# Root mean squares of five norms through split sums and Ln/Exp instead of Sqrt, reciprocal and a diagonal tile

## The chip, the cores and the metric

The kernel runs on one core of a Trainium2 chip. The metric is the device time of one execution, in microseconds. Five engines matter: TensorE (PE; its weight loads are listed as PEld), VectorE (DVE), ScalarE (ACT), GpSimd (POOL) and SyncE (SP). Each works through its own instructions in order, and they wait for each other through semaphores. DMAs are issued from the queues of SP, ACT and POOL.

## The reference

A residual stream x of 1024 tokens by 1024 features passes through two layers. Layer 0 mixes with a short gated convolution, layer 1 with dilated attention, and after each comes a SwiGLU FFN. A root-mean-square norm stands ahead of each of these four parts, and a fifth at the end:

```python
def rms_norm(x, g):
    xf = x.astype(jnp.float32)
    y = xf * lax.rsqrt(jnp.mean(xf * xf, axis=-1, keepdims=True) + EPS)
    return (y * g.astype(jnp.float32)).astype(x.dtype)

def reference(x, mix_norm, ffn_norm, final_norm, ...):
    for i in range(DEPTH):
        h = rms_norm(x, mix_norm[i])
        if i % N_MIXERS == 0:
            x = x + short_conv_mixer(h, conv_w_in[j], conv_kernel[j], conv_w_out[j])
        else:
            x = x + dilated_attention_mixer(h, attn_w_qkv[j], attn_w_out[j], rel_bias)
        h = rms_norm(x, ffn_norm[i])
        x = x + swiglu(h, ffn_w_gate[i], ffn_w_up[i], ffn_w_down[i])
    return rms_norm(x, final_norm)
```

All of it is float32. Per token the norm needs one number, 1/rms (called rstd below).

## The kernel before

Activations lie transposed: a tile has 128 features on its partitions and the tokens along its columns, so x is eight tiles of 128x1024. [...]

Every dense product keeps float32 precision with split operands: a tile t becomes a high part (a copy by ScalarE into the rounded type fp32r, L142) and a low part (t minus the high part, by VectorE, L143), and a product is three matmuls, high by high, high by low and low by high (L570 to L572 in `mm`, L370 to L372 in `product`). A further scheme, in the manner of Strassen and Winograd (class `Strassen`), makes seven block products out of eight; the sums of blocks that it needs are VectorE's work (L190), as are the sums of its results (L580), while ScalarE saves banks to tiles (L576).

The order of the work is written out by hand. `unit_order` lists the products of a stage; after each product a callback (`start`, `filled`, `idle`) issues a fixed portion of the other engines' work, and `ensure` splits weights a few products ahead. The engines then run in that order, and instructions wait where their data are not there. Tiles come from pools: 41 pages of 128x1024, and half tiles of 128x512 (20 of them in the first and third part of the kernel, 8 in the attention), which hold the parts of products, block sums and other passing tiles.

A norm runs in these steps. ScalarE squares x tile by tile, and the squares are added into one tile `acc` of 128x1024 by VectorE (L445) or by adding DMAs. `Norm.stats` (L464) then works in two steps, around a `yield`:

- First step. For each 128 tokens TensorE multiplies `acc` (as weights) by one column of ones (L471), which gives the sums over features with the tokens on the partitions. ScalarE takes Sqrt (L474), VectorE the reciprocal (L475), and VectorE multiplies an identity tile `eye` by it (L480), which gives diagonal tiles `diag`, 512 columns each.
- Second step. TensorE multiplies ones by `diag` in full float32 (L487), which brings 1/rms of every token to all partitions, and ScalarE copies it to `rstd` (L488).

The conv stage calls both steps for all 1024 columns at once (`gather` and `spread`, after the products (0,3) and (2,5)) and then squares rstd (L1106), which VectorE's next work needs. The query/key stage does the same after (1,2) and (3,1). Each FFN has a first half in `group1` and a second half in `feed_forward` (n == key+1 and key+2), after which `second_half` makes VectorE and ScalarE build operands from rstd (L1276, L562), and ScalarE loads the table for Silu (L1364). The attention scales its value products by `norm.r`, the small tile with tokens on the partitions (L1517).

The last norm stands in `final`. The last product group runs over column pieces of 512, 256 and 256 tokens, eight tiles n each. After each tile VectorE adds the product to x (L492), ScalarE squares it (L1957) and multiplies by the gain (L1959), and `between` adds squares and, for the piece before, issues `squared_sum` at n == 1 and `spread` at n == 3; then `some(1)` scales a finished tile by rstd (L1968) and sends it out. For the last piece the last square is summed by TensorE itself (L1984), and VectorE multiplies by the bank (L1997) directly.

ScalarE's functions come from tables, and a change of table is an instruction of its own. Three places call Sqrt or Silu on one column only to have the table there early (L1364, L1708, L2005).

Of the kernel before, what the change touches and what calls it, by code (L numbers as in the profile page):

```python
# [10 lines left out]
F32 = mybir.dt.float32  # L11
# [6 lines left out]
S = 1024  # L18
D = 1024
# [12 lines left out]
WARM = 10  # L32

# [65 lines left out]
def trunk(ctx: ExitStack, tc: tile.TileContext, x, gains_in, cwi, ck, cwo, wqkv, wo, relb,  # L99
# [27 lines left out]
    eye = consts.tile([128, 128], F32)  # L127
# [267 lines left out]
    class Norm:  # L395
# [68 lines left out]
        def stats(self, c0, c1):  # L464

            self.flush()
            w = c1 - c0
            nt = w // 128
            b = bank()
            for t in range(nt):  # L470
                nc.tensor.matmul(b[:, t:t + 1], self.acc[:, c0 + 128 * t:c0 + 128 * t + 128], ones[:, 0:1],  # L471
                                 start=True, stop=True)
            r = self.r = consts.tile([128, KT], F32, name="r", tag="r", bufs=2)
            nc.scalar.activation(r[:, :nt], b[:, :nt], AF.Sqrt, scale=1.0 / D, bias=eps)  # L474
            nc.vector.reciprocal(r[:, :nt], r[:, :nt])  # L475
            diags = []
            for p0 in range(0, nt, 4):
                n = min(4, nt - p0)
                diag = half_page("diag")
                nc.vector.tensor_tensor(out=view(diag, 0, [[128, n], [1, 128]]),  # L480
                                        in0=view(eye, 0, [[0, n], [1, 128]]),
                                        in1=view(r, p0, [[1, n], [0, 128]]), op=ALU.mult)
                diags.append((c0 + 128 * p0, 128 * n, diag))
            yield
            for p0, n, diag in diags:
                b = bank()
                nc.tensor.matmul(b[:, :n], ones, diag[:, :n], start=True, stop=True)  # L487
                nc.scalar.activation(self.rstd[:, p0:p0 + n], b[:, :n], AF.Copy)  # L488
# [8 lines left out]
    def bias_tables():  # L497
# [30 lines left out]
        nc.vector.tensor_tensor(out=d, in0=d, in1=m, op=ALU.subtract)  # L528
        nc.scalar.activation(d, d, AF.Exp)
# [590 lines left out]
    class QueryKey(Conv):  # L1120
# [43 lines left out]
        def mix(self):  # L1164
# [44 lines left out]
            def spread():  # L1209
                run(stats)  # L1210
                self.ready = True
# [263 lines left out]
    def attention(norm, qk):  # L1475
# [193 lines left out]
        def finish(p):  # L1669
# [211 lines left out]
    nc.scalar.dma_start(gains, gains_in)  # L1881

# [27 lines left out]
    nc.gpsimd.dma_start(eye, ident)  # L1910
    nc.vector.memset(ones, 1.0)
    nc.vector.memset(eps, EPS)
# [165 lines left out]
```

## Time and profile before

| | us |
|---|---|
| median of 3 runs | 2137.89 |
| lowest and highest run | 2135.56, 2138.65 |
| profiled execution | 2136.81 |
| its span | 2135.0 |
| TensorE busy | 2103.4 (99%) |
| VectorE busy | 1744.7 (82%) |
| ScalarE busy | 1009.2 (47%) |
| GpSimd busy | 256.5 (12%) |

The granted clock of TensorE is 0.996 over the span. In rows in order of time the first two numbers are an instruction's start and duration in us; behind the engine and the line stand the operation, what it writes and reads, and the shape. In square brackets is the time that the engine idled before it, and what it waited for. Rows with `x8` merge several instructions. A full float32 matmul shows as two records. In rows of groups the busy time and the mean in ns of one instruction follow the bar.

### The profile page before, as it was taken

The page shows a single profiled execution, that of the slowest core. Times are in us where ns is not written, and L with a number is a line of the kernel's source. Part 1 is how long each engine was busy: PE and PEld are TensorE (multiplying, and loading weights), DVE is VectorE, ACT ScalarE, POOL GpSimd, SP SyncE. Part 2 cuts the span into 40 slices and gives each one's busy share as a digit, 9 for nine tenths or more (in the row PEclk, how much of TensorE's full clock was granted, in tenths as well). Part 3 has the DMA queues.
Part 4 walks back from the last instruction along what each step waited for, and adds up shares of the span by engine and source line. Part 5 has one row for each costly group of instructions (what it writes and reads, how often), then busy time and mean ns, then how long its engine had stood idle before and what let it go on. Part 6 is the DMA issues. An engine that isn't in the chain of part 4 may idle for free. (4 is left out here: it accounts for less than half of the span.)

```text
span 2135.0 us, 31015 instructions
## 1 busy us (share of the span) xinstructions
PE 2103.4 (99%) x11082; PEld 1805.6 (85%) x11082; DVE 1744.7 (82%) x3273; ACT 1009.2 (47%) x1853; POOL 256.5 (12%) x375
## 2 busy tenths in 40 slices
PE   9999999999999999999999999999999999999998
PEld 7788888888888888877899998888788888888887
DVE  8898769988888888868967687777998888888876
ACT  7333426443444554446545544545543434456435
POOL 1000000110101000010322333221011101001000
PEclk9999999999999999999999999999999999999999
DMA  7322642333332576340767777765123333368432
GB/s 219 94 94 70 227 137 71 104 104 104 114 109 99 170 218 197 112 167 30 265 204 182 186 194 216 214 198 160 59 94 105 103 109 113 101 199 240 157 94 79
DMA packets 143449, 304.90 MB, mean 143 GB/s; under 512 B 48972, under 2 KB 55422, under 8 KB 143296
## 3 DMA queue, kind: packets, MB, share of 16 engines
q1 hardware_dynamic: 107488, 201.94, 31.5%
q0 software_dynamic: 28176, 86.29, 12.7%
q10 hardware_dynamic: 7632, 14.70, 1.8%
q8 instruction: 88, 1.44, 0.3%
q14 instruction: 65, 0.53, 0.1%
HBM read 212.48 MB, written 83.05 MB: 138 GB/s over the span
## 5 line engine op out<-in xcount | busy, mean ns | idle before, releaser
L572 PE MATMUL bank<-b,w 128*128 128x512 f32 x1952 | 760.9, 390 | 4.9 <-DVE w L143 4.7
L570 PE MATMUL bank<-b,w 128*128 128x512 f32 x1952 | 762.8, 391 | 2.5 <-ACT w L142 1.7
L571 PE MATMUL bank<-b,w 128*128 128x512 f32 x1952 | 760.4, 390 | 0.6 <-DVE b L881 0.6
L572 PEld LDWEIGHTS bank<-b,w 128*128 128x128 f32 x1952 | 366.4, 188 | 85.8 <-DVE w L143 9.6
L570 PEld LDWEIGHTS bank<-b,w 128*128 128x128 f32 x1952 | 366.7, 188 | 79.5 <-ACT w L142 2.8
L571 PEld LDWEIGHTS bank<-b,w 128*128 128x128 f32 x1952 | 366.7, 188 | 76.0 <-DVE b L881 1.2
L142 ACT ACTIVATE w<-combo 128x512 fp32r<-128x512 f32 (+2 forms) x488 | 249.1, 540 | 231.5 <-DVE combo L190 214.6
L143 DVE TENSOR_TENSOR w<-combo,w 128x512 fp32r<-128x512 f32 (+2 forms) x488 | 276.2, 579 | 37.8 <-ACT w L142 37.1
L576 ACT ACTIVATE part<-bank 128x512 f32<-128x512 f32 x186 | 110.8, 596 | 388.8 <-PE bank L572 385.3
L143 DVE TENSOR_TENSOR w<-raw,w 128x512 fp32r<-128x512 f32 (+2 forms) x342 | 189.6, 575 | 38.6 <-ACT w L142 38.6
L580 DVE TENSOR_TENSOR part<-part,bank 128x256 f32<-128x256 f32 (+1 forms) x366 | 170.5, 495 | 31.2 <-PE bank L572 16.7
L142 ACT ACTIVATE w<-raw 128x512 fp32r<-128x512 f32 (+2 forms) x342 | 166.7, 530 | 44.9 <-PE bank L572 12.2
L370 PE MATMUL bank<-w_hi,w 128*128 128x512 f32 (+1 forms) x400 | 153.3, 383 | 5.1 <-ACT w_hi L142 3.7
L371 PE MATMUL bank<-w_lo,w 128*128 128x512 f32 (+1 forms) x400 | 149.7, 374 | 1.2 <-DVE w_lo L143 1.2
L372 PE MATMUL bank<-w_hi,w 128*128 128x512 f32 (+1 forms) x400 | 149.7, 374 | 0.7 <-DVE w L143 0.7
L800 DVE TENSOR_TENSOR x<-x,bank 128x512 f32<-128x512 f32 x136 | 92.6, 681 | 29.2 <-PE bank L572 29.0
L492 DVE TENSOR_TENSOR x<-x,bank 128x512 f32<-128x512 f32 (+1 forms) x104 | 66.1, 641 | 56.6 <-PE bank L372 56.1
L190 DVE TENSOR_TENSOR combo<-raw 128x512 f32<-128x512 f32 (+1 forms) x172 | 111.1, 646 | 0.0
L370 PEld LDWEIGHTS bank<-w_hi,w 128*128 128x128 f32 x400 | 75.8, 189 | 18.5 <-ACT w_hi L142 3.9
L371 PEld LDWEIGHTS bank<-w_lo,w 128*128 128x128 f32 x400 | 75.7, 189 | 14.9 <-DVE w_lo L143 2.0
L372 PEld LDWEIGHTS bank<-w_hi,w 128*128 128x128 f32 x400 | 75.6, 189 | 14.8 <-DVE w L143 1.6
L563 DVE TENSOR_TENSOR b<-hin,b 128x512 fp32r<-128x512 f32 x126 | 79.5, 684 | 9.4 <-ACT b L562 9.4
(252 smaller groups left out, 3488.6 us busy)
## 6 DMA issues: line engine op xcount, KB each, us to landing
hin<-part SPq DMA_DIRECT2D x126, 256.0 KB
raw<-in_ffn_w_gate SPq DMA_DIRECT2D x44, 512.0 KB
raw<-in_ffn_w_up SPq DMA_DIRECT2D x44, 512.0 KB
part<-sum POOLq DMA_DIRECT2D x72, 256.0 KB, 2.3
raw<-in_ffn_w_down SPq DMA_DIRECT2D x48, 384.0 KB
raw<-in_attn_w_qkv SPq DMA_DIRECT2D x27, 512.0 KB
raw<-in_conv_w_in SPq DMA_DIRECT2D x24, 512.0 KB
part<-part POOLq DMA_DIRECT2D x36, 256.0 KB, 2.4
```

What stands on the lines that cost most here:

```text
L142: nc.scalar.activation(hi, src, AF.Copy)
L143: eng.tensor_tensor(out=lo, in0=src, in1=hi, op=ALU.subtract)
L190: eng.tensor_tensor(out=c, in0=a, in1=b, op=op)
L370: nc.tensor.matmul(b, whi[:, a], ahi[:, s], start=first, stop=False)
L371: nc.tensor.matmul(b, whi[:, a], alo[:, s], start=False, stop=False)
L372: nc.tensor.matmul(b, wlo[:, a], ahi[:, s], start=False, stop=last)
L570: nc.tensor.matmul(b, hi[:, a], bhi, start=start and k == 0, stop=False, skip_group_check=True)
L571: nc.tensor.matmul(b, hi[:, a], blo, start=False, stop=False, skip_group_check=True)
L572: nc.tensor.matmul(b, lo[:, a], bhi, start=False, stop=k == n - 1, skip_group_check=True)
L576: nc.scalar.activation(t, b, AF.Copy)
L580: nc.vector.tensor_tensor(out=t, in0=t, in1=b, op=ALU.add)
L800: nc.vector.tensor_tensor(out=X[n][:, half(h)], in0=X[n][:, half(h)], in1=b, op=ALU.add)
```

## The change

`stats` splits `acc` into high and low parts per 512 columns instead of summing it by TensorE. The second step, `spread_sums`, multiplies a 128x128 tile of ones in fp32r by both parts into one bank, which puts the sums over features on all partitions at once; ScalarE makes rstd from it as Ln, then Exp of -1/2 of that. Reciprocal, `diag` and the identity go. The table set that is named for Ln and Exp is loaded at the start, ahead of the Exp in `bias_tables`, and in `final`; the early Sqrt calls go. The query/key norm writes one row of rstd to DRAM and gathers it back with tokens on the partitions, for the attention's `norm.r`. In `final`, the last piece's sums up to tile 6 are split before the last tile, the last square behind it, and four matmuls add them up.

```diff
+    ones_r = consts.tile([128, 128], F32R)
-    eye = consts.tile([128, 128], F32)
...
         def stats(self, c0, c1):
             self.flush()
-            for t in range(nt):
-                nc.tensor.matmul(b[:, t:t + 1], self.acc[:, c0 + 128 * t:c0 + 128 * t + 128], ones[:, 0:1],
-                                 start=True, stop=True)
-            r = self.r = consts.tile([128, KT], F32, name="r", tag="r", bufs=2)
-            nc.scalar.activation(r[:, :nt], b[:, :nt], AF.Sqrt, scale=1.0 / D, bias=eps)
-            nc.vector.reciprocal(r[:, :nt], r[:, :nt])
...
-            for p0, n, diag in diags:
-                b = bank()
-                nc.tensor.matmul(b[:, :n], ones, diag[:, :n], start=True, stop=True)
-                nc.scalar.activation(self.rstd[:, p0:p0 + n], b[:, :n], AF.Copy)
+            parts = []
+            for p0 in range(c0, c1, HALF):
+                s = slice(p0, min(p0 + HALF, c1))
+                w = s.stop - s.start
+                parts.append((s, split(self.acc[:, s], [half_page("sum", F32R)[:, :w] for _ in range(2)])))
+            yield
+            for s, sums in parts:
+                spread_sums(self.rstd[:, s], [sums])
+
+    def spread_sums(rstd, sums):
+        w = rstd.shape[1]
+        b = bank()[:, :w]
+        terms = [t for pair in sums for t in pair]
+        for i, t in enumerate(terms):
+            nc.tensor.matmul(b, ones_r, t, start=i == 0, stop=i == len(terms) - 1)
+        nc.scalar.activation(rstd, b, AF.Ln, scale=1.0 / D, bias=eps)
+        nc.scalar.activation(rstd, rstd, AF.Exp, scale=-0.5)
...
         nc.vector.tensor_tensor(out=d, in0=d, in1=m, op=ALU.subtract)
+        nc.scalar.preload_act_table_set(LN_EXP)
         nc.scalar.activation(d, d, AF.Exp)
...
                 run(stats)
+                rms = dram.tile([1, S], F32, name="rms")
+                norm.r = consts.tile([128, KT], F32, name="r")
+                nc.gpsimd.dma_start(rms, norm.rstd[0:1, :])
+                nc.gpsimd.dma_start(norm.r, bass.AP(rms.tensor, rms.offset, [[1, 128], [128, KT]]))
...
-                    nc.scalar.activation(scratch, eps, AF.Sqrt)
...
     nc.scalar.dma_start(gains, gains_in)
+    nc.scalar.preload_act_table_set(LN_EXP)
...
-    nc.gpsimd.dma_start(eye, ident)
+    nc.vector.memset(ones_r.bitcast(F32), 1.0)
...
+            def parts(t, i):
+                s = slice(*pieces[i])
+                w = s.stop - s.start
+                return split(t[:, s], [half_page("sum", F32R)[:, :w] for _ in range(2)])
...
             def between(i, n):
-                add_squares(int(n > 0))
+                add_squares(int(n > 0 and (i, n) != (len(pieces) - 1, KT - 2)))
                 if (i, n) == (0, 5):
-                    nc.scalar.activation(scratch, eps, AF.Sqrt)
+                    nc.scalar.preload_act_table_set(LN_EXP)
                 if i and n == 1:
-                    diags.append(squared_sum(i - 1))
+                    known.append(parts(norm.acc, i - 1))
                 elif i and n == 3:
                     s = slice(*pieces[i - 1])
-                    nc.scalar.activation(norm.rstd[:, s], spread(diags.pop()), AF.Copy)
+                    spread_sums(norm.rstd[:, s], [known.pop()])
                     scale.extend((i - 1, k, norm.rstd[:, s]) for k in range(KT))
+                elif i == len(pieces) - 1 and n == KT - 2:
+                    known.append(parts(norm.acc, i))
                 some(1)
...
             last = len(pieces) - 1
-            add_squares(1)
-            diag = squared_sum(last, sums.pop()[0])
+            known.append(parts(sums.pop()[0], last))
             some(KT)
-            rstd = spread(diag)
+            rstd = norm.rstd[:, slice(*pieces[last])]
+            spread_sums(rstd, known)
             for n in range(KT):
                 scaled(last, n, rstd)
```

`LN_EXP` is the string "natural_log_exp_and_others".

More of the change, by code (lines that the diff above doesn't have):

```diff
@@ L32 @@
 WARM = 10
+LN_EXP = "natural_log_exp_and_others"
 def paired(pairs, chunk, tiles):
@@ L1994, in spread @@
-            def spread(diag):
-                b = bank()
-                w = diag.shape[1]
-                nc.tensor.matmul(b[:, :w], ones, diag, start=True, stop=True)
-                return b[:, :w]
-            diags = []
+            def parts(t, i):
+                s = slice(*pieces[i])
+                w = s.stop - s.start
+                return split(t[:, s], [half_page("sum", F32R)[:, :w] for _ in range(2)])
+            known = []
             def between(i, n):
-                add_squares(int(n > 0))
+                add_squares(int(n > 0 and (i, n) != (len(pieces) - 1, KT - 2)))
```

28 lines of the change are left out of this document (removed).

## The prediction

> **What bounds the kernel now.** I read the busy times on the page first, then the waits of TensorE, then busy time by stretch, and then the order of time round each norm.
>
> ```profile
> PE 2103.4 (99%) x11082; PEld 1805.6 (85%) x11082; DVE 1744.7 (82%) x3273; ACT 1009.2 (47%) x1853; POOL 256.5 (12%) x375
> ```
>
> ```profile
> PE bank L572 <- DVE w L143: 4.7, 6, 1.7
> ```
>
> ```profile
> 360.00:380.00 20.00, 20.00 (x89) 16.54 (x89) 20.00 (x34) 12.27 (x23) 0.77 (x2) 1.00 0.16 40
> ...
> 1020.00:1040.00 20.00, 19.42 (x83) 15.35 (x83) 19.93 (x32) 10.39 (x18) 7.44 (x14) 1.00 0.72 250
> ...
> 1520.00:1540.00 20.00, 19.02 (x84) 15.21 (x83) 20.00 (x34) 11.68 (x21) 1.68 (x3) 1.00 0.35 119
> ```
>
> TensorE (PE) is busy for 99% of the span, and its largest wait for another engine sums to 4.7 us over the whole kernel. So a TensorE instruction that goes is worth its time, as long as the others keep up. The stretches (columns: length, then busy time of PE, PEld, DVE, ACT, POOL) show where that is doubtful: behind the norms VectorE (DVE) works 19.93 to 20.00 us of 20, and in two of these three stretches TensorE is already short of full (19.42 and 19.02). ScalarE (ACT) has room everywhere.
>
> **What TensorE gives back.** These are TensorE's rows round the norms: first the conv norm, then the norm of the first FFN, then that of the second.
>
> ```profile
> 66.72 0.39 PE L572 MATMUL bank<-b,w 128*128 128x512 f32 x1
> ...
> 68.97 0.40 PE L571 MATMUL bank<-b,w 128*128 128x512 f32 x1
> ...
> 76.72 0.40 PE L572 MATMUL bank<-b,w 128*128 128x512 f32 x1
> ...
> 78.90 0.40 PE L571 MATMUL bank<-b,w 128*128 128x512 f32 x1
> ```
>
> ```profile
> 313.42 0.39 PE L372 MATMUL bank<-w_hi,w 128*128 128x512 f32 x1
> ...
> 315.10 0.39 PE L371 MATMUL bank<-w_lo,w 128*128 128x512 f32 x1
> ...
> 340.01 0.39 PE L572 MATMUL bank<-b,w 128*128 128x512 f32 x1
> ...
> 341.90 0.40 PE L571 MATMUL bank<-b,w 128*128 128x512 f32 x1
> ```
>
> ```profile
> 1496.75 0.39 PE L571 MATMUL bank<-b,w 128*128 128x512 f32 x1
> 1496.97 0.39 PE L572 MATMUL bank<-b,w 128*128 128x512 f32 x1
> 1497.20 0.95 PE L471 MATMUL bank<-ones,acc 128*128 128x1 f32 x8
> ...
> 1498.33 0.40 PE L571 MATMUL bank<-b,w 128*128 128x512 f32 x1
> ...
> 1500.65 0.40 PE L572 MATMUL bank<-b,w 128*128 128x512 f32 x1
> 1500.88 1.02 PE L487 MATMUL bank<-diag,ones 128*128 128x512 f32 x2
> ...
> 1501.98 0.40 PE L571 MATMUL bank<-b,w 128*128 128x512 f32 x1
> ```
>
> Dense matmuls on split operands start 0.22 to 0.23 us apart (1496.75, 1496.97, 1497.20); I use 0.23. From an L572 to the next-but-one product would be two steps, 0.46. What is more than that is the norm's own time. The sums of 512 columns cost 1498.33-1496.97-0.46 = 0.90, and the spread (L487, full fp32) 1501.98-1500.65-0.46 = 0.87. In their place come two split-operand matmuls of 128x512, 2 x 0.23 = 0.46. So 512 columns give TensorE 0.90+0.87-0.46 = 1.31 us.
>
> Conv, both halves at once: 2.25-0.46 = 1.79 for the sums, 2.18-0.46 = 1.72 for the spread, less 4 x 0.23: 2.59. The query/key norm has the same instructions, 2.59. First FFN: its sums took 1.68-0.46 = 1.22 and 1.89-0.46 = 1.43, waits for the last squares included, which go with them; with two spreads, 1.22+1.43+2x0.87-2x0.46 = 3.47. Second FFN: 2 x 1.31 = 2.62. Final norm, pieces of 512 and 256 before the tail: 1.31+0.65 = 1.96. TensorE's bill falls by 13.2 us.
>
> **What the reader of rstd sees.** The chain after the spread gets longer:
>
> ```profile
> 1501.94 0.60 ACT L488 ACTIVATE rstd<-bank 128x512 f32<-128x512 f32 x1 [2.97 <-PE bank L487]
> ...
> 1502.57 0.69 DVE L1276 TENSOR_TENSOR x<-x,rstd 128x512 f32<-128x512 f32 x1 [1.26 <-ACT rstd L488]
> ```
>
> ```profile
> L1632 ACT ACTIVATE lh<-lh 128x512 f32<-128x512 f32 x16 | 9.8, 615 | 0.0
> L1268 ACT ACTIVATE x<-x,gains 128x512 f32<-128x512 f32 x8 | 5.7, 708 | 0.0
> ```
>
> Before, rstd is there 1502.54-1500.88 = 1.66 after the first spread matmul starts. Ln has a bias column, so I take L1268's 0.71 for it; Exp of this size is L1632's 0.62. The second matmul starts 0.23 after the first and lasts 0.39; ACT follows a PE end by 0.04 (1501.90 to 1501.94). So 0.62+0.04+0.71+0.04+0.62 = 2.03, 0.37 later. Ln and Exp stand in line: each needs the one before.
>
> VectorE loses the reciprocal and the diag tile's 128x512 product, and gains the low part, a subtraction of the same shape and so of the same price. ScalarE gets a copy at Exp's 0.62, Ln and Exp for a small Sqrt and a copy of 0.60: at most 1.35 more per 512 columns. With ScalarE at 47% that alone costs nothing; where it counts is the 0.37.
>
> **What of it reaches the end, norm by norm.** Second FFN: the rows of 1502.57 and of 1520 to 1540 say that VectorE starts its operands when rstd comes, is full, and has TensorE waiting for it. So rstd decides, not TensorE: the first half moves it 1.31 forward, the second half's dropped sums 0.90, less 0.37: 1.84 (ends 1.84 and 2.62, TensorE's own).
>
> ```profile
> 346.13 2.50 DVE L1276 TENSOR_TENSOR x<-x,rstd 128x512 f32<-128x512 f32 x4 [0.84 <-ACT rstd L488]
> ```
>
> ```profile
> 983.46 1.28 ACT L474 ACT_TABLE_LOAD   x1
> ...
> 985.05 0.20 DVE L475 RECIPROCAL r<-r 128x8 f32<-128x8 f32 x1 [0.89 <-ACT r L474]
> ```
>
> ```profile
> 1004.63 1.41 DVE L881 SCALAR_TENSOR_TENSOR b<-x,gains,b 128x512 fp32r<-128x512 f32 x2 [1.15 <-ACT b L880]
> ```
>
> ```profile
> 1020.53 0.50 PE L572 MATMUL bank<-b,w 128*128 128x512 f32 x1 [0.46 <-DVE w L143]
> ```
>
> First FFN: rstd moves 1.22+0.87-0.46+1.43-0.37 = 2.69; TensorE 3.47 and, in 360 to 380, without a wait. The low end is what VectorE can give: 1.22-0.37 = 0.85 from the first half, the reciprocal's 0.20, and the 0.84 it idles: 1.9. I take 2.5, between, nearer to rstd's.
>
> Query/key: at 1020.53 TensorE waits for VectorE, so VectorE must move too. Its idle time before, 0.89 at 985.05 (behind the table load of 1.28, which goes) and 1.15 at 1004.63, plus the 0.20 reciprocal, allow 2.24; the low end, without the second idle time, is 1.1, the high end TensorE's 2.59. I take 2.2.
>
> Conv: VectorE's next work waits for a square of the whole rstd, and so for both halves. The second half's rstd now takes 2.03+0.04+0.71+0.04+0.62 = 3.44 from the first spread matmul; it took about 2 x 0.87+0.2+0.60 = 2.54. That is 0.9 later, so 1.79-0.9 = 0.9 at worst; TensorE gives 2.59 and never waits there. I take 2.4.
>
> ```profile
> 2107.94 0.69 DVE L1968 TENSOR_TENSOR x<-x,rstd 128x512 f32<-128x512 f32 x1 [1.17 <-ACT rstd L2010]
> ...
> 2121.27 0.42 DVE L1968 TENSOR_TENSOR x<-x,rstd 128x256 f32<-128x256 f32 x1 [1.02 <-ACT rstd L2010]
> ...
> 2124.99 0.42 DVE L492 TENSOR_TENSOR x<-x,bank 128x256 f32<-128x256 f32 x1 [0.30 <-PE bank L372]
> ...
> 2129.13 2.74 DVE L1968 TENSOR_TENSOR x<-x,bank 128x256 f32<-128x256 f32 x8
> ```
>
> ```profile
> 2125.45 0.42 ACT L1957 ACTIVATE sq<-x 128x256 f32<-128x256 f32 x1 [0.43 <-DVE x L492]
> 2125.90 0.51 ACT L1959 ACTIVATE x<-x,gains 128x256 f32<-128x256 f32 x1
> ```
>
> Final norm: here TensorE's 1.96 is lost. VectorE carries the pieces, and waits for rstd at 2107.94 and 2121.27; both waits grow by about 0.37. Before the last L492 there are now an add that waits for the square just begun, a wait for the high part, and the low part (0.3 issue): about 1.1. Two reciprocals (0.37) go, and some of the wait for each Sqrt, since TensorE is no longer in that chain (I estimate 0.4 together). 1.1+0.74-0.37-0.4 = 1.1: so much later comes the last L492. From there to the first of the last eight products it was 2129.13-2124.99 = 4.14; now: square at +0.46, gain at +0.91, the copy at +1.33 for 0.42, the low part to +2.22, matmuls to +2.55, Ln of 256 (as L1959, 0.51) to +3.10, Exp 0.42 to +3.56: 0.6 shorter. Together 0.5 later; I take a gain of -0.5, with ends -1.0 (no idle time absorbs any) and +2.0 (TensorE's).
>
> **Edits at nothing.** The load of the identity goes and a memset of ones comes ahead of any data. On the POOL queue the row and the gather of rms come in front of the stores of the query/key stage:
>
> ```profile
> 1020.91 0.59 POOL L1144 DMA_DIRECT2D kq<-kq_hi  x1 [74.22 <-ACT w L142]
> ```
>
> The queue was idle for 74.22 us until then, and rstd is there some ten us after the reciprocal at 985.05. So both transfers have some 25 us before they hold up a store, and the gathered rows are read only behind this stage. SP's queue is not touched. Of the table loads, those that a Sqrt needed go; but for the one at 983.46 they lie in idle time of ScalarE.
>
> [...] A table load takes 1.28 here and the next instruction starts at once:
>
> ```profile
> 353.12 1.28 ACT L1364 ACT_TABLE_LOAD   x1
> 354.41 0.20 ACT L1364 ACTIVATE scratch<-eps 128x1 f32<-128x1 f32 x1
> ```
>
> [...]
>
> **The sum.** 2.4+2.5+2.2+1.84-0.5 = 8.4 us off the profiled execution's 2136.81 (span 2135.0): 2128.4. That execution lies 1.1 under the median of the runs, 2137.89. The low ends, 0.9+1.9+1.1+1.84-1.0 = 4.7, give 2132.1; the high ends, 2.59+3.47+2.59+2.62+2.0 = 13.3, give 2123.5.
>
> **Rivals.** *TensorE alone decides* (2123.5): VectorE keeps up everywhere and the tail gains. For it: 99% against 82%, and hardly a wait. Against it: the three full stretches, and the wait at 1020.53.
>
> *VectorE decides* (2132.1): each norm gives only its low end. For it: stretches at 20.00 of 20. Against it: TensorE waits in them for no more than 1 us, so some slack is there.
>
> *Slower: ScalarE changes its table between Ln and Exp.* The trace shows the danger: an Exp and the Ln right behind it each needed a load of their own.
>
> ```profile
> L529 ACT ACT_TABLE_LOAD x1 | 1.3, 1283 | 0.0
> L530 ACT ACT_TABLE_LOAD x1 | 1.3, 1283 | 0.0
> ```
>
> If the set named at the start does not stay for both, 512 columns cost two loads, 2.57 us, in the chain from the spread to rstd. It counts where VectorE waits for rstd: the second half of both FFN norms and the three pieces of the last norm, 5 x 2.57 = 12.9, and up to 23 with the first halves and conv. 2128.4+12.9 to 2128.4+23 is 2141 to 2151; I take 2144. From seven loads in these places (8.4/1.28 = 6.6) the change loses. Against it: the change loads a set by name, where before the choice was free. [...]
>
> *It gains nothing* (2137): each 512 columns now hold two half tiles from the split to the spread, where one diag tile was held, out of a pool of 20 in which the products' parts live too. A product that waits for a free one could give the 8.4 back. No row shows how full the pool is.
>
> **How the numbers follow.** Less than 0.2% (4.3 us) can hardly be told from no change here. Forecast 0.58, TensorE alone 0.12, VectorE 0.13, nothing gained 0.08, table changes 0.09. The predicted time is the forecast's, 2128.4. Faster takes the forecast, TensorE alone and most of VectorE's case (below 2133.6): 0.80. Same: 0.09, from nothing gained and the slow edge of VectorE's case. Slower: 0.11, the table changes and the worst of the waits for a half tile. The range goes from 2122.5, a little past TensorE's end, to 2136.0, into the case without a gain; outside stay the table changes and some of the rest.
>
> **What would show it.** Right: two matmuls 0.23 apart in each half's place and none in the sums' place; one table load ahead of the first norm, none between Ln and Exp; about 0.37 more from the first spread matmul to rstd; a larger wait of TensorE for VectorE in the second FFN's start, 1.0 us to some 1.8; the last tile's L492 nearly as late as before. Wrong: loads between Ln and Exp; waits for half tiles round the norms; a store of keys later than 1020 behind the gather; TensorE gaining more than 2.59 at conv or less than 1.84 at the second FFN.

## The result and the profile after

| | before | after |
|---|---|---|
| median of 21 runs each, us | 2138.33 | 2134.95 |
| ratio, with its 95% interval | 1 | 0.9987 [0.998, 0.9994] |
| profiled execution, its span, us | 2136.81, 2135.0 | 2135.06, 2133.1 |
| TensorE busy, us | 2103.4 | 2096.6 |
| TensorE matmul records | 11082 | 11000 |

The kernel became faster, by 0.13% by the ratio and by 3.4 us between the medians. The forecast was 2128.4, some 8 to 10 us less than before. So the sign is right, the time lies in the range, and well over half of the gain is missing.

The page of the changed kernel has these busy times:

```profile
PE 2096.6 (98%) x11000; PEld 1800.6 (84%) x11000; DVE 1743.4 (82%) x3266; ACT 1013.7 (48%) x1861; POOL 257.4 (12%) x376
```

These are the stretches behind the three norms that the prediction showed of before, now of the changed kernel (columns: length, busy time of PE, PEld, DVE, ACT, POOL, granted clock, DMA share, GB/s):

```profile
360.00:380.00 20.00, 20.00 (x90) 16.57 (x89) 20.00 (x34) 12.58 (x24) 1.68 (x3) 1.00 0.28 88
1020.00:1040.00 20.00, 20.00 (x88) 16.20 (x88) 19.97 (x31) 10.70 (x19) 7.04 (x14) 1.00 0.76 252
1520.00:1540.00 20.00, 19.29 (x84) 15.79 (x85) 19.97 (x35) 11.20 (x22) 2.22 (x4) 1.00 0.38 132
```

They hardly moved. What TensorE waits for, over the whole changed kernel (line, releaser, us in total, times, longest), is where the loss shows:

```profile
PE bank L1570 <- ACT o L1667: 5.8, 4, 2.5
...
PE bank L482 <- ACT sum L143: 4.4, 3, 2.1
PE bank L569 <- DVE w L144: 3.8, 6, 1.1
...
PE bank L482 <- DVE sum L144: 1.3, 1, 1.3
```

The matmul of ones (now L482) waits 5.7 us for the high and low parts of the sums, about 1.9 in the first FFN and 3.7 in the last norm. The sums and spreads in whose place it stands waited 2.1 before (L471, L1982 and L1997: 0.3, 0.8 and 1.0). (In the changed kernel L143 is the high part, L144 the low part, L445 the Square, L446 the adding of squares, L191 a block sum, L483 Ln, L484 Exp, L488 the adding to x, L567 to L569 the dense products, L1969 the products of the last norm and L1970 its output DMAs.)

To see stage by stage where the time went I laid the same instructions of two traces beside each other and followed by how much the later one is ahead. The second column of numbers is the difference of the two first traces, the third the mean of three traces of the changed kernel less the mean of four of the kernel before (minus is faster):

| stage | forecast | first pair | means |
|---|---|---|---|
| start | 0 | -0.2 | -0.5 |
| conv | -2.4 | -2.6 | -2.6 |
| first FFN | -2.5 | +0.6 | +0.1 |
| bias tables | 0 | -1.2 | -1.3 |
| query/key | -2.2 | -2.1 | -2.1 |
| attention | 0 | +2.2 | +1.9 |
| second FFN | -1.84 | -1.1 | -1.1 |
| last norm | +0.5 | +2.5 | +2.5 |
| sum | -8.4 | -1.9 | -3.1 |

Conv and query/key came as forecast. Five terms did not: the first FFN, the attention, the last norm, part of the second FFN, and, to the good, the bias tables.

### The profile page after: what moved, and what is told of

Its sections match the earlier page's. It is cut to its first block, busy times and chain, and to the rows that moved or that the text cites. A ratio compares the mean times of both kernels' runs of the same rounds, so it can differ in the third digit from the quotient of the medians.

```text
span 2133.1 us, 30849 instructions
## 1 busy us (share of the span) xinstructions
PE 2096.6 (98%) x11000; PEld 1800.6 (84%) x11000; DVE 1743.4 (82%) x3266; ACT 1013.7 (48%) x1861; POOL 257.4 (12%) x376
## 3 DMA queue, kind: packets, MB, share of 16 engines
q8 instruction: 87, 1.43, 0.3%
## 4 chain that ended last, share of the span: by engine, by line
PE 41%; DVE 7%; issue 2%; ACT 2%; POOL 1%; DMA 1%; SPq 0%; DVEq 0%; ACTq 0%; POOLq 0%
PE bank L569 8%; PE bank L568 8%; PE bank L567 8%; PE bank L1643 3%; PE bank L372 2%; PE bank L373 2%; PE bank L371 2%; PE bank L659 1%; PE bank L662 1%; PE bank L661 1%; PE bank L1513 1%; PE bank L1514 1%; PE bank L1515 1%; POOL mb L1624 1%; PE bank L1571 1%
## 5 line engine op out<-in xcount | busy, mean ns | idle before, releaser
L569 PE MATMUL bank<-b,w 128*128 128x512 f32 x1952 | 761.8, 390 | 4.0 <-DVE w L144 3.8
L567 PE MATMUL bank<-b,w 128*128 128x512 f32 x1952 | 762.3, 391 | 2.8 <-ACT w L143 2.2
L569 PEld LDWEIGHTS bank<-b,w 128*128 128x128 f32 x1952 | 367.1, 188 | 84.6 <-DVE w L144 8.2
L567 PEld LDWEIGHTS bank<-b,w 128*128 128x128 f32 x1952 | 367.5, 188 | 79.6 <-ACT w L143 3.1
L143 ACT ACTIVATE w<-combo 128x512 fp32r<-128x512 f32 (+2 forms) x488 | 249.2, 540 | 232.6 <-DVE combo L191 214.2
L144 DVE TENSOR_TENSOR w<-combo,w 128x512 fp32r<-128x512 f32 (+2 forms) x488 | 277.8, 583 | 37.8 <-ACT w L143 37.0
L144 DVE TENSOR_TENSOR w<-raw,w 128x512 fp32r<-128x512 f32 (+2 forms) x342 | 190.6, 579 | 38.4 <-ACT w L143 38.4
L143 ACT ACTIVATE w<-raw 128x512 fp32r<-128x512 f32 (+2 forms) x342 | 166.9, 530 | 46.0 <-PE bank L569 11.5
L191 DVE TENSOR_TENSOR combo<-raw 128x512 f32<-128x512 f32 (+1 forms) x172 | 111.8, 650 | 0.0
L488 DVE TENSOR_TENSOR x<-x,bank 128x512 f32<-128x512 f32 (+1 forms) x104 | 66.3, 643 | 55.6 <-PE bank L373 55.3
```

The lines of the kernel that those rows point to most:

```text
L143: nc.scalar.activation(hi, src, AF.Copy)
L144: eng.tensor_tensor(out=lo, in0=src, in1=hi, op=ALU.subtract)
L191: eng.tensor_tensor(out=c, in0=a, in1=b, op=op)
L567: nc.tensor.matmul(b, hi[:, a], bhi, start=start and k == 0, stop=False, skip_group_check=True)
L569: nc.tensor.matmul(b, lo[:, a], bhi, start=False, stop=k == n - 1, skip_group_check=True)
```

## The experiments

The gains below are read in the same way, each kernel's trace against the first trace of before.

### What the chip itself scatters

The same two kernels, profiled again, so that a difference of one pair isn't taken for an effect.

> The changed kernel once more. By the two traces at hand it gained 3.0 us at the conv norm, 1.2 at the bias tables and 2.1 at the query/key norm, and gave back 0.6 at the start, 0.6 at the first FFN's norm, 2.2 within the attention and 2.2 in the last norm. Theory: the start and the attention are chance of one execution, and come out otherwise here (attention within 1 us of the length it had before), while the losses at the first FFN (0.6) and in the last norm (2.2) come again to within 0.2. Rival: the attention's loss belongs to the change (its r comes by a gather now) and comes again with 2 us or more.

> The kernel before, for one more trace of its start, its conv stage and its attention. Theory: its first trace had a short start and a short attention by chance; here the start is 0.3 to 0.8 us and the attention 0.5 to 3 us longer than there. Rival: only the changed kernel's attention is long; here start and attention are as in the first trace to within 0.4.

> A further trace of the kernel before; as for before_1. By the theory the attention's length differs from trace to trace by 1 us and more in either kernel; by the rival it repeats to within 0.4.

> A further trace of the kernel before; as for before_1. With six traces of the same attention and eleven of the changed kernels' the means can be set side by side: by the theory they lie within 1 us, by the rival 2 us or more apart.

> A third trace of the changed kernel. Theory: attention anywhere from 0.3 to 3.7 us over the first trace of the kernel before, the first FFN's norm at -0.7 or +0.7 according to whether the clock falls behind the wait, the last norm 2.2 longer as ever. Rival: the attention repeats the 2.2 and 3.4 of the first two traces to within 0.6.

Timed, the changed kernel came to 2135.52, ratio 0.998 [0.997, 0.9989]. Spans were 2135.1 and 2128.9 for the changed kernel, 2136.2, 2133.9 and 2136.8 for the one before. Within one kernel three stages scatter and the others repeat within 0.1: the start (the traces of before differ by 1.9 at 200 us; the changed kernel's stand at -0.2, +0.7 and -0.1), the attention (from 2.2 shorter to 1.5 longer than in the first trace of before, and in the changed kernel from 0.3 shorter to 3.4 longer), and, in the changed kernel alone, the first FFN (+0.6, +0.6, -1.05). So a difference at the start is chance. Conv gave 2.6 and the last norm lost 2.5 in each of the three; the 0.6 at the start, the 3.0 at conv and the 2.2 in the last norm that the expectations take are each off by 0.3 to 0.8.

### The first FFN: who waits for the split

In the changed kernel ScalarE's order in the first half, the first 512 tokens, is: Square of the newest tile, copy of the sums, Square of the next tile, Ln, Exp. ScalarE's rows of the changed kernel:

```profile
311.76 0.63 ACT L445 ACTIVATE acc<-x 128x512 f32<-128x512 f32 x1 [2.09 <-DVE x L488]
...
312.30 0.61 ACT L143 ACTIVATE sum<-acc 128x512 fp32r<-128x512 f32 x1
316.20 0.63 ACT L445 ACTIVATE acc<-x 128x512 f32<-128x512 f32 x1 [3.29 <-DVE x L488]
...
316.74 0.67 ACT L483 ACTIVATE rstd<-bank,eps 128x512 f32<-128x512 f32 x1
317.44 0.63 ACT L484 ACTIVATE rstd<-rstd 128x512 f32<-128x512 f32 x1
```

And VectorE's, of the same time:

```profile
312.95 0.69 DVE L144 TENSOR_TENSOR sum<-acc,sum 128x512 fp32r<-128x512 f32 x1 [1.22 <-ACT sum L143]
...
315.49 0.68 DVE L488 TENSOR_TENSOR x<-x,bank 128x512 f32<-128x512 f32 x1
318.11 0.75 DVE L1247 SCALAR_TENSOR_TENSOR hcol<-x,gains,rstd 128x512 f32<-128x512 f32 x1 [1.94 <-ACT rstd L484]
```

ScalarE idles 3.29 us and Ln then starts at once behind the Square, with no wait of its own: it stood in the queue behind a Square that waits for VectorE's L488, three block sums after the low part. Ln's bank was there at 314.19, 2.55 earlier:

```profile
313.56 0.63 PE L482 MATMUL bank<-sum,ones_r 128*128 128x512 f32 x2
```

VectorE, which is the pace here, idles 1.22 and then 1.94. The kernel before had the same order, with its copy to rstd behind that Square:

```profile
318.85 0.63 ACT L444 ACTIVATE acc<-x 128x512 f32<-128x512 f32 x1 [3.50 <-DVE x L492]
...
319.56 0.60 ACT L488 ACTIVATE rstd<-bank 128x512 f32<-128x512 f32 x1
```

So there too VectorE's x released rstd, and not TensorE. From the Square's start to rstd it was 1.31 (318.85 to 320.16) and is now 1.87 (316.20 to 318.07), since Ln and Exp stand where one copy stood. In the second half TensorE has the wait. Its rows:

```profile
339.37 0.50 PE L482 MATMUL bank<-sum,ones_r 128*128 128x512 f32 x1 [0.64 <-ACT sum L143]
341.13 0.71 PE L482 MATMUL bank<-sum,ones_r 128*128 128x512 f32 x1 [1.26 <-DVE sum L144]
341.63 0.63 PE L567 MATMUL bank<-b,w 128*128 128x512 f32 x1
342.06 0.63 PE L568 MATMUL bank<-b,w 128*128 128x512 f32 x1
```

Two things are seen: 1.9 us of waiting, and after it matmuls of 0.63 instead of 0.39, 0.43 apart instead of 0.23. The stretches of the first and the third trace of the changed kernel (columns: length, PE busy, granted clock, DMA share, GB/s) tell these apart:

```profile
340.00:344.00 4.00, 2.87 (x7) 0.66 0.25 43
344.00:348.00 4.00, 4.00 (x17) 0.92 0.00 0
```

```profile
340.00:344.00 4.00, 2.89 (x13) 1.00 0.25 43
344.00:348.00 4.00, 4.00 (x19) 1.00 0.02 4
```

The same wait, once with the clock granted falling to 0.66 and once without. In the first trace it is one stretch of 3.41 us at half clock, which starts 0.12 us behind the second wait's end:

```profile
341.25:344.66 3.41, 3.41 (x9) 0.50 0.00 0
```

The clock's loss is 4 x 0.34 + 4 x 0.08 = 1.7 us, and the first FFN of the two traces differs by 1.7 (+0.6 against -1.05).

Three edits try the explanation. The first moves copy, Ln and Exp ahead of the Square, in the callback that runs before it:

```diff
 # group1, added(...)
+                if j and n == i:
+                    pre.append(norm.stats(0, HALF))
+                    next(pre[0])
+                elif j and n == i + 1:
+                    run(pre.pop())
+                    pre.append(sw.first_half())
 # group1, between(...)
                 if n == i:
-                    pre.append(norm.stats(0, HALF))
-                    next(pre[0])
                     for m in (6, 7):
                         combos[i, 0](m)
-                elif n == i + 1:
-                    run(pre.pop())
-                    pre.append(sw.first_half())
```

> The changed kernel with the copy of the sums, and later Ln and Exp, issued ahead of the square of the tile at hand in the first half of both FFN norms. Theory: in ScalarE's order they stand behind a square that waits for VectorE, and VectorE then waits 1.2 us for the copy and 1.5 to 1.9 for rstd; those waits go, VectorE's chain of operands moves 1.2 to 2 us forward, and of that at least 1 us reaches the end at the first FFN. Rival: VectorE's chain has room and only TensorE's matmuls count, so the time moves by less than 0.4.

The second leaves the first half and starts the second half's split earlier, ahead of VectorE's block sums:

```diff
                     last_step()
+                    next(stats)
                     for m in (6, 7):
                         combos[self.key, 1](m)
...
                 if n == self.key + 1:
-                    next(stats)
```

> The changed kernel with the split of the sums of the second half of both FFN norms issued right behind the last squares, ahead of three block sums on VectorE. Theory: TensorE's wait of 1.9 us for the split at the first FFN goes, and with it the lower clock behind it (0.66 to 0.77 granted for 4 us); the first FFN's norm then gains 0.7 to 1.5 where it lost 0.7, and no stretch behind it falls below a clock of 0.98. Rival: VectorE's order alone decides, rstd comes at most 0.3 earlier at its reader, and the norm still loses 0.4 or more.

The third asks whether TensorE's own work counts here at all. It gives the two FFN norms their sums by one column of ones back, into a bank that nobody reads; the output is computed as in the changed kernel.

```diff
             yield
+            # ahead of this yield, for the FFN norms only:
+            if self.g in (2, 3):
+                b = bank()
+                for t in range((c1 - c0) // 128):
+                    nc.tensor.matmul(b[:, t:t + 1], self.acc[:, c0 + 128 * t:c0 + 128 * t + 128], ones[:, 0:1],
+                                     start=True, stop=True)
```

> The changed kernel with the old one-column matmuls of the sums put back on TensorE in the FFN norms, to no use: 2 x 0.9 us of its work for each FFN. Theory: at the first FFN TensorE waits 1.9 us for the split anyhow, so the work fills the wait, nothing is lost there, and the clock does not fall; at the second FFN, where rstd decides, less than 0.5 is lost. Rival: TensorE's own work counts, and each FFN's norm gets 1.8 us longer.

| kernel | ratio | first FFN | clock 340 to 348 | second FFN |
|---|---|---|---|---|
| changed, three traces | 0.9987 [0.998, 0.9994] | +0.6, +0.6, -1.05 | 0.66/0.92, 0.80/0.77, 1.00 | -1.1 |
| copy, Ln, Exp ahead of the Square | 0.9953 [0.9939, 0.9968] | -3.5 | 1.00 | -2.0 |
| split earlier | 0.998 [0.9971, 0.9989] | -0.9 | 1.00 | -0.8 |
| sums back | 1.0001 [0.9992, 1.001] | +1.9 | 0.57/1.00 | 0.0 |

Ahead of the Square, VectorE's wait for rstd falls from 1.94 to 0.74 and TensorE waits for no sums at all; the first row is ScalarE's, the second VectorE's, of that kernel:

```profile
314.56 0.69 ACT L483 ACTIVATE rstd<-bank,eps 128x512 f32<-128x512 f32 x1 [1.89 <-PE bank L482]
```

```profile
315.94 0.75 DVE L1247 SCALAR_TENSOR_TENSOR hcol<-x,gains,rstd 128x512 f32<-128x512 f32 x1 [0.74 <-ACT rstd L484]
```

Ln now waits for TensorE, as the forecast had it, and the first FFN gains 3.5, all of TensorE's 3.47. That settles the cause: the queue's order, and not VectorE's work, which is the same (busy 1743.7 us for 1743.4). The second half gains by it too: VectorE comes to its low part at 338.22 instead of 340.39, and TensorE finds both parts there. With the split earlier TensorE's second-half wait shrinks to

```profile
339.44 0.51 PE L482 MATMUL bank<-sum,ones_r 128*128 128x512 f32 x1 [0.53 <-ACT sum L143]
340.17 0.50 PE L482 MATMUL bank<-sum,ones_r 128*128 128x512 f32 x1 [0.22 <-DVE sum L144]
```

and the clock is 1.00 in that trace. But the gain is only the 0.9 that the third trace had without the edit, and at 366.48 TensorE waits 0.89 for a low part of VectorE's instead. So 1.15 us less of waiting bought nothing by itself, and whether the edit keeps the clock up one trace can't tell; the first half's loss remains. With the sums given back the first FFN ends 1.9 behind the kernel before, 1.3 to 3.0 behind the changed one, and the second FFN gains nothing for its 1.1. I had expected less, since VectorE seemed to set the pace: TensorE's own work counts for more than I held, though in the first FFN a wait of 1.37 and a clock of 0.57 came with it, so that this stage doesn't tell the two apart.

### The last norm: a queue again

ScalarE's rows at the end of the changed kernel:

```profile
2123.37 0.40 ACT L143 ACTIVATE sum<-sq 128x256 fp32r<-128x256 f32 x1
2124.93 1.01 ACTq L1970 DMA_DIRECT2D out<-x  x2
2125.99 0.47 ACT L483 ACTIVATE rstd<-bank,eps 128x256 f32<-128x256 f32 x1 [2.22 <-DVE x L1969]
2126.49 0.42 ACT L484 ACTIVATE rstd<-rstd 128x256 f32<-128x256 f32 x1
```

TensorE's last sums start at 2123.82 and take 1.04, so the bank is there at 2124.86. Ln starts 1.13 later, released by VectorE's x: two output DMAs stand ahead of it in ScalarE's queue, and wait for VectorE's products. Before, VectorE read the bank itself, and behind the last Square nothing of ScalarE's stood in that chain but a Sqrt. One edit puts the spread ahead of those products, another gives the last norm its old form back (one-column sums, Sqrt, reciprocal, diagonal tile), with the other four norms new:

```diff
 # spread first
-            some(KT)
             rstd = norm.rstd[:, slice(*pieces[last])]
             spread_sums(rstd, known)
+            some(KT)
```

```diff
 # old last norm
-            known.append(parts(sums.pop()[0], last))
+            add_squares(1)
+            diag = squared_sum(last, sums.pop()[0])
             some(KT)
-            spread_sums(rstd, known)
+            rstd = spread(diag)
```

> The changed kernel with the last piece's matmuls, Ln and Exp issued ahead of the remaining products of the piece before (whose output transfers ScalarE issues). Theory: Ln sits in ScalarE's queue behind transfers that wait for VectorE's products, so that it starts 1.1 us after its matmul's end; without them it starts within 0.1 and the end comes 1.0 to 1.2 earlier. Rival: VectorE's own products, which come behind in either order, decide, and the end moves by less than 0.3.

> The change in the first four norms, the last norm as it was. Theory: the last norm alone costs 2.2 us, so its stretch is as long as before, and the kernel is 2 us faster than the changed one. Rival: the end of the kernel is set by the output's transfers, which start no earlier, and the gain is under 0.7.

With the spread first Ln follows TensorE, and the DMAs stand behind it:

```profile
2123.04 0.47 ACT L483 ACTIVATE rstd<-bank,eps 128x256 f32<-128x256 f32 x1 [1.13 <-PE bank L482]
2123.55 0.42 ACT L484 ACTIVATE rstd<-rstd 128x256 f32<-128x256 f32 x1
2123.61 3.53 ACTq L1970 DMA_DIRECT2D out<-x  x6
```

The last norm then loses 1.55 instead of 2.5; ratio 0.9969 [0.9956, 0.9982]. With the old form it loses 0.4, ratio 0.9965 [0.9952, 0.9977]. So 1.0 was the queue, and 1.1 the longer chain. The 0.4 that the old form still loses comes behind its last add, which stands 3.51 earlier than before (2121.48 for 2124.99), as much as the work ahead of the last norm; the section on the 32 bytes comes back to it.

### A table load that was counted at nothing

The kernel before, with the set of Ln and Exp named ahead of the Exp of the bias tables, and nothing else changed:

```diff
+        nc.scalar.preload_act_table_set("natural_log_exp_and_others")
         nc.scalar.activation(d, d, AF.Exp)
```

> The kernel before with one line of the change: the set of tables for both Ln and Exp, named ahead of the Exp in bias_tables. Theory: one of the two table loads there goes, and with it 1.2 to 1.3 us of TensorE's wait of 1.34 for the weights that ScalarE splits behind it; the rest of the trace stays, so 1.2 us less by that stretch. Rival, as predicted: loads lie in idle time of ScalarE and the stretch does not move. The run is also a second sample of the old start and the old attention: if these are as long as in the four traces of changed kernels (0.4 to 0.8 longer at the start, 0.8 to 3.4 in the attention), the change has no part in them.

It gains 1.25 between 480 and 960 us, all of the 1.2 to 1.3 that the changed kernel gains there. The row of before that shows why is TensorE's, behind ScalarE's two loads of L529 and L530 (1.28 each):

```profile
946.22 0.50 PE L370 MATMUL bank<-w_hi,w 128*128 128x512 f32 x1 [1.34 <-ACT w L142]
```

The changed kernel has no such wait. Timed, the ratio is 0.9993 [0.9984, 1.0002]: 1.2 us are too few to be told by the time alone.

### The attention, and 32 bytes

The attention isn't touched, yet it lasts longer in eleven of the twelve traces of changed kernels than in the first of before. One suspect came from the memory's layout. The change drops one of two small buffers of 32 bytes (`r`), which by the order of the program lies ahead of all large pages, so that each moves by 32 bytes (no trace shows the addresses). Between 1060 and 1460 us a packet of 256 bytes takes 23 ns on the mean instead of 19; one of 1024 bytes, which only the last norm's outputs have, takes 49 instead of 46. The DMA share rises from 0.71 to 0.75 (columns as above; first before, then the changed kernel):

```profile
1060.00:1460.00 400.00, 388.59 (x2729) 0.99 0.71 201
```

```profile
1060.00:1460.00 400.00, 387.76 (x2719) 0.98 0.75 198
```

Two kernels test it from both sides, one giving the changed kernel the 32 bytes back, the other taking 32 from the kernel before:

```diff
 # 32 bytes back, in the changed kernel
-                norm.r = consts.tile([128, KT], F32, name="r")
+                norm.r = consts.tile([128, KT], F32, name="r", tag="r", bufs=2)
 # 32 bytes less, in the kernel before
-    eps = consts.tile([128, 1], F32)
-    scratch = consts.tile([128, 1], F32)
+    two = consts.tile([128, 2], F32, name="two")
+    eps, scratch = two[:, 0:1], two[:, 1:2]
```

> The changed kernel with the small tile r in two buffers again, as before; nothing else. Theory: the change dropped one buffer of 32 bytes per partition, so every page and half tile behind it lies 32 bytes lower, and the DMAs that touch them take longer: packets of 256 bytes 23 ns where it was 19, of 1024 bytes 49 where it was 46. That costs the attention, which waits for DMAs, 0.8 to 3.7 us. With the 32 bytes back the packets take 19 and 46 again, the mean DMA share between 1060 and 1460 us falls from 0.74 to 0.71, and the attention is again as long as before to within 0.5: some 2 us less than the changed kernel. Rival: the gather of r or its place in DRAM slows the attention, and packets and attention stay as in the changed kernel.

> The kernel before with two one-column tiles of constants in one, which takes 32 bytes per partition from in front of the pages; no instruction changes. Theory: its packets of 256 bytes take 23 ns instead of 19, its attention gets 0.8 to 3.7 us longer, and the kernel 1 to 3.5 slower. Rival: no change at all, under 0.5 us.

The packets follow the 32 bytes exactly: 19 ns and a share of 0.70 with them back, 23 ns and 0.75 in the kernel before without them. Why they take longer then isn't shown. But the attention doesn't follow: it stays 3.4 longer with the bytes back, and in the kernel before without them it is 2.1 longer, where that kernel's own traces run from -2.2 to +1.5. The layout isn't the cause. Nor does the whole time follow: 0.998 [0.9971, 0.9989] with the bytes back, as without; 1.0006 [0.9996, 1.0015] for the kernel before without them.

At the very end the traces do show a cost, too small for those intervals. Of the kernel before, four further traces with the 32 bytes end their last norm as the first does, to within 0.02; without them it lasts 0.41 longer, and so it does in all four kernels that have the old last norm and new ones ahead of it (0.40 to 0.41). The changed kernel with the bytes back loses 2.3 there instead of 2.5. The last thing in this stage is the output's DMAs, with the packets of 1024 bytes.

What the rows do show is a TensorE that comes earlier and finds ScalarE not ready. This is TensorE in the second trace of the changed kernel:

```profile
1242.35 0.38 PE L1570 MATMUL bank<-qa,ka 128*128 128x256 f32 x1 [2.51 <-ACT o L1667]
...
1244.61 0.63 PE L371 MATMUL bank<-b,w_hi 128*128 128x512 f32 x1
1245.03 0.63 PE L372 MATMUL bank<-b,w_hi 128*128 128x512 f32 x1
```

In the first trace of before this place has no wait. ScalarE's Exp that leads to it (first before, then the first trace of the changed kernel) came 1.6 earlier, while TensorE started the same matmul shortly ahead of the wait 4.2 earlier (1237.75 for 1241.94):

```profile
1238.22 1.06 ACT L1632 ACTIVATE lf<-lf 128x1024 f32<-128x1024 f32 x1 [3.37 <-DVE lf L1631]
```

```profile
1236.62 1.06 ACT L1633 ACTIVATE lf<-lf 128x1024 f32<-128x1024 f32 x1 [3.37 <-DVE lf L1632]
```

And as in the first FFN the granted clock falls behind the wait (the stretch of two waits, before and then the second trace of the changed kernel):

```profile
1165.00:1300.00 135.00, 131.98 (x947) 1.00 0.75 198
```

```profile
1165.00:1300.00 135.00, 132.49 (x932) 0.97 0.76 188
```

In there this trace has two stretches of 3.41 us at half clock, from 1165.05 and 1243.55, so 3.4 us of clock, and from 1100 to 1300 it loses 4.4. Over all traces: six of the kernel before and its variants show 1.00 in this stretch and differ from the first by -1.9 to +1.2 (mean +0.1); of twelve of changed kernels ten show less than 1.00, and the stretch from 1100 to 1300 is longer by 0.3 to 4.4 (mean 2.2). So the loss is hardly chance alone, and the waits and the clock go with it. They aren't all of it: the kernels with the split earlier and with the sums back keep 1.00 and still lose 3.6 and 3.2. No edit here moved this wait alone, so the cause is read from rows and not proved. GpSimd's and VectorE's rows, first of before and then of the first trace of the changed kernel, show where the chain falls behind TensorE:

```profile
1210.40 0.58 POOL L1677 DMA_DIRECT2D zc<-zdram  x1 [3.69 <-DMA zdram<-z]
...
1216.41 1.22 DVE L1631 TENSOR_TENSOR lf<-lf,mb 128x1024 f32<-128x1024 f32 x1 [3.45 <-POOL mb L1623]
```

```profile
1208.79 0.57 POOL L1678 DMA_DIRECT2D zc<-zdram  x1 [6.36 <-DMA zdram<-z]
...
1214.80 1.22 DVE L1632 TENSOR_TENSOR lf<-lf,mb 128x1024 f32<-128x1024 f32 x1 [6.11 <-POOL mb L1624]
```

GpSimd issues the store of `z` 4.3 earlier (1201.86 for 1206.14), but then waits 6.36 instead of 3.69 for it to land, and `mb`, which stands behind it in GpSimd's queue, lets VectorE go only 1.6 earlier. Why that store takes longer to land stays open.

### Put together

The old last norm, with copy, Ln and Exp ahead of the Square in the first FFN; then the same with another 32 bytes moved, and that with the split earlier too:

> The new norm in the first four places, with the steps of the FFN's first half ahead of the square, and the last norm as it was. If the parts add up as the traces say, 5.4 us from the moved steps and 2.2 from the old last norm: about 2128 against a changed kernel of 2135.5, 0.995 of the kernel before. If the old last norm only helped because of what stood around it, 2130 or more.

> The new norm in four places with the moved steps, the old last norm, and 64 instead of 32 bytes less in front of the pages. Theory: what counts is the remainder by 64 bytes, so packets of 256 bytes take 19 ns, the attention is as long as before, and the kernel comes to 0.3 to 2 us under the one without it (ratio 0.9951). Rival: any shift of the pages slows the packets: no gain.

> The same with the split of the second half's sums ahead of three block sums as well. At the second FFN rstd decides, and it moves up to 0.7 earlier: 0 to 0.7 us less than without. Rival: VectorE's order decides and nothing moves.

| kernel | median, us | ratio |
|---|---|---|
| old last norm, ahead of the Square | 2126.52 | 0.9951 [0.9939, 0.9964] |
| the same, 32 bytes moved | 2128.38 | 0.9954 [0.9941, 0.9966] |
| and the split earlier | 2129.22 | 0.9955 [0.9942, 0.9969] |

All three are the same within their intervals, and beat both kernels: some 0.45 to 0.5% under before, the change as given being 0.13 to 0.2% under it. In the first the first FFN gains 3.5, the second 1.9, and the last norm loses 0.4 instead of 2.5. The time alone can't tell it from the kernel with the steps ahead of the Square and the new last norm (0.9953). No gain was seen from the earlier split on top, nor from the bytes: with another 32 moved a packet of 256 bytes still takes 22 ns, so the remainder by 64, which stood as a theory before that run, isn't what counts.

## Why the prediction was right and wrong

*TensorE's bill* was right. Two matmuls stand in each half's place, 0.23 apart, and nothing where the sums were; conv gave 2.6 in every trace for 2.4, all of TensorE's 2.59 and, within the reading, not more; query/key gave 2.1 for 2.2, and the first FFN the full 3.5 once its queue was mended.

*The chain to rstd* was right: Ln 0.67 to 0.69, Exp 0.63, Exp 0.03 behind Ln, for the 0.71 and 0.62 taken; where nothing stands ahead of Ln, in the second half of the second FFN, rstd is there 2.03 after the first spread matmul (1496.04 to 1498.07), as summed. *The rival of table changes* is out. There is no load between Ln and Exp; of ten loads five are left, the one of the Exp of the bias tables among them:

```profile
L1365 ACT ACT_TABLE_LOAD x2 | 2.6, 1283 | 0.0
L1882 ACT ACT_TABLE_LOAD x1 | 1.3, 1283 | 1.2 <-PEq L2048 1.2
L525 ACT ACT_TABLE_LOAD x1 | 1.3, 1283 | 0.0
L1986 ACT ACT_TABLE_LOAD x1 | 1.3, 1283 | 0.0
```

Behind the load of L525 (939.87) Exp and Ln of the bias tables follow each other (941.62 and 941.90) with none between, where before the Ln had its own load of 1.28 (L530, 944.10).

*The step that failed* is "First FFN: rstd moves 1.22+0.87-0.46+1.43-0.37 = 2.69". It took rstd of the first half to move with TensorE, and Ln to start when the bank is there. On ScalarE "47% busy" hid that its queue stood still: Ln was behind a Square that waited for VectorE, as the copy to rstd had been before, so what TensorE saved there could not move it. rstd came at 318.07 (317.44+0.63) for 320.16 before, 2.09 earlier, where VectorE's adds just before had been 2.81 earlier already (L488 at 311.04 for L492 at 313.85), so 0.7 was lost where the forecast's low end alone had 0.85 of gain. In the second half TensorE, which the forecast had never wait for the split, waited 1.9 us, and in some executions the clock then fell, worth 1.7. The 2.5 became nothing. "With ScalarE at 47% that alone costs nothing" is the sentence at fault: ScalarE's room was real, its order wasn't looked at.

*Second FFN*: 1.1 for 1.84. Right in kind; the order of copy, Ln and Exp ahead of the Square, which works in both FFNs, gave it 2.0, so the term was lowered by the same queue and not by VectorE's work.

*Last norm*: a loss of 2.5 for 0.5. Before the last add it was 1.5 for the 1.1 taken: the add stood 2.98 earlier than before (2122.01 for 2124.99), where VectorE's adds ahead of the first piece's sums had been 4.45 earlier (2097.79 for 2102.24). What failed most is "0.6 shorter" from there on: 2126.94 - 2122.01 = 4.93 for the old 4.14, so 0.8 longer. The working went step by step through the operations and left out the output DMAs that ScalarE's queue issues between them, 1.13 of the 1.4; the other 0.3 is the matmuls, whose bank came 2.85 behind the add for 2.55. The last 0.3 of the loss lies behind the last add's chain, in the outputs. The sign "the last tile's L492 nearly as late as before" did not follow from the sum itself, by which that add comes 8.94 - 1.1 = 7.8 earlier.

*Edits at nothing*: right for the row and its gather on the POOL queue, which go out at 990 and 993, 20 us ahead of the first store of keys. Wrong for the tables: the working counted only the loads that a Sqrt needed. Of the two loads of the bias tables, which it shows under its rivals, one goes as well, and with it TensorE's wait of 1.34 at 946.22, so that 1.25 came as a gain.

*Rivals*: "TensorE alone" describes the mended first FFN, not the change as given. "VectorE decides" named the right engine to watch but the wrong reason: VectorE waited, it didn't run out. Waits for half tiles weren't seen. That a stage without any edit, the attention, would give 2 us back stood in no rival.

## What to carry to other kernels

A busy share tells what an engine could do, its queue tells when: ScalarE was busy for 48% of the span, and Ln stood 2.55 us behind its bank in the first FFN. Where a change puts new links of a chain on an engine with room, write down what stands ahead of each link in that engine's order, DMA issues included, and what those wait for. A TensorE that gains time ahead of others may spend it waiting, as the 1.9 us in the first FFN show, and can pay for the wait a second time, as with the 1.7 us when the granted clock fell behind it.

## What the runs showed of the hardware that was not expected

Waits of TensorE of about 1.9 us were followed, in four traces of six, by a fall of its clock that cost 1.7 us more. The six hold the change's first FFN without an edit there, with its two waits (0.64 and 1.26 in the first trace); in four the clock of the eight us round and behind them was between 0.66 and 0.92 and the stage lost 0.55 to 0.63, in two it stayed at 1.00 and the stage gained 1.0 and 1.05. Whether it falls differs between executions of the same kernel. In the first trace the fall is the stretch of 3.41 us at 0.50, with matmuls 0.43 apart instead of 0.23. What decides whether it comes isn't shown.

With 32 bytes less in front of the pages packets of 256 bytes took 23 ns instead of 19, and those of 1024 bytes 49 instead of 46. That the pages move by them follows from the order of the program and shows in no trace. By the traces the 32 bytes cost this kernel 0.25 to 0.4 us at the end, where the last outputs leave; the times alone could not tell it.
